# Two-layer diffusion step on one core: the second layer's feed-forward up product in seven block products instead of eight, and slabs of one size

## The chip, the cores and the metric

One core of a Trainium2 chip runs the whole program. The metric is the device time of one execution in microseconds (us), median of several runs. Engines: PE is TensorE (PEld its weight loads), DVE VectorE, ACT ScalarE, POOL GpSimd, SP the queue that issues DMAs.

## The reference, cut to what matters

A backbone of two layers works on 128 context and 512 latent tokens, 640 in all, of 1024 features. Each layer has attention, a state-space scan (SSD) and, at its end, the feed-forward part that the change is about:

```python
D_MODEL = 1024; SEQ = 128; DEC_SEQ = 512; DEPTH = 2; D_FF = 2816; FFN_CONV = 3
...
    x = x + g1 * (merged @ p['w_out'])
    h = modulate(x, sh2, sc2)
    u = dw_conv(h @ p['w_up'], p['ffn_conv_w'], p['ffn_conv_b'])
    u_val, u_gate = jnp.split(u, 2, axis=-1)
    x = x + g2 * ((jax.nn.silu(u_gate) * u_val) @ p['w_down'])
```

`w_up` is 1024 by 5632 (u_val and u_gate, 2816 each), and `dw_conv` is a convolution of width three over tokens, per feature. Inputs and outputs are float32.

## The kernel before, in words

All products run on PE in float32 split in two parts: `split` makes a rounded high part (a CAST on ACT) and the rest (a subtraction on DVE), and each product of two split operands takes three matmuls (high·high, high·low, low·high).

Nothing is issued where it is written. The functions record operations on tiles in a `Flow`, whose list scheduler then orders each engine's operations: an operation is taken when its dependences and buffers allow, among several by the rank of its class (`RANK`: "f" for the main stream, "d" for work done beside it, "m" for the modulation), and at equal rank as recorded. Each engine then runs its rows in that fixed order. So all instructions of the trace carry one line, L178 (L182 after), and a row is known by its tiles: `pf`, `p`, `pp` are PSUM banks, `wr`/`wh`/`wl` a raw weight tile and its high and low part, `slab` the large buffers for tokens, `tmp` smaller ones, `fw` the convolution's weights and biases.

Feature-major products (`feat_half`) hold a weight tile of 128 x 128 in PE and stream tokens: 640 tokens lie in 642 padded columns, in halves of 386 and 256. Token-major ones (`tok_major`) hold tokens and stream 512 columns of weights.

The feed-forward part has 22 feature tiles for u_val and 22 for u_gate. `up_item(p, jl)` is one **unit**: two tiles (a = 0, 1) of each matrix (s = 0 for u_val, 1 for u_gate), two halves: 8 groups of 24 matmuls. Behind a group `conv_in` takes it out of PSUM with two ACT rows; behind two, `conv_taps` adds the neighbours (two DVE rows of 642); for s = 1 `silu2` and a multiplication gate the pair, and a split writes the product into the g slabs. Units come in three stages, **up 0** (four units), **up 1** (four) and **up 2** (three), each followed by `down_item(p, 0)` and `(p, 1)`, together **down p**, which multiplies the gated features with `w_down` in 240 matmuls of 512 columns (180 in down 2). Weights of a unit are two tiles of 128 x 2048 (`w_feat`, 1 MB each), loaded and split by `wprep` two specs ahead, in rings of two `wr` and three each of `wh` and `wl`.

Ahead of up 0 stands `w_out_item`: per token tile it updates x, normalises it (`norm_tile`), transposes it on PE, and `norm_mod` scales, shifts and splits it into four slabs of two sizes that all units read. Slabs of a second kind (`slabd`, NSLABD = 5 of them) carry g, the scan's B and C, and other things.

Of the kernel before, what the change touches and what calls it, by code (L numbers as in the profile page):

```python
# [18 lines left out]
P = 128  # L19
# [9 lines left out]
NSLABD = 5  # L29
# [11 lines left out]
def _mask(dims, cache={}):  # L41
    """Bits of the free elements that an access pattern touches."""
# [299 lines left out]
def hybrid_step_kernel(  # L342
# [25 lines left out]
    def slab(h, shape, dt=F32):  # L368
        return flow.tile(slabs, shape, dt, f"slab{h}", nm("slab"), 2)
# [98 lines left out]
    def wprep(parts, wide=False):  # L468
        parts, scales = parts if isinstance(parts, tuple) else (parts, None)
# [32 lines left out]
    # token-major product: stationary tokens, moving weights of 512 columns  # L502
# [16 lines left out]
    # tokens in two parts: tiles 0 to 2 and tiles 3 and 4  # L519
    def part(i):  # L520
        return (0, col(i)) if i < 3 else (1, col(i) - HOFF[1])

    def tile_h(hT, i):
        h, o = part(i)
        return lambda a, kt: hT[a][h][:, kt, o:o + P]

    # tokens that wait in DRAM: two quads of feature tiles, in pieces of four, tile after tile
    def tok_load(src, q0):
# [3 lines left out]
        def load(n):  # L532
            for _ in range(n):
                i = len(tiles)
                while len(pieces) < 4 * i + 4:
                    h, k = (0, 6) if len(pieces) < 12 else (1, 4)
                    t = slab(h, [P, k, 4, P], F32R)
                    pieces.extend(t[:, j] for j in range(k))
# [33 lines left out]
    def norm_x(xh, xns, junk):  # L572
        """Both halves of a token tile over their root mean square."""
# [15 lines left out]
    def norm_mod(src, h, i, n, modT, hT, on_act):  # L589
# [8 lines left out]
        b, o = part(i)  # L598
        ks = slice(4 * n, 4 * n + 4)
        split(hT[0][b][:, ks, o:o + P], hT[1][b][:, ks, o:o + P], h)  # L600

    def norm_tile(x0, x1, t, i, modT, hT):
        """x0 and t are written over."""
        xns = [x0, t]
        norm_x([x0, x1], xns, t)
        for n in range(2):
            h = xns[n].rearrange("p (k t) -> p k t", k=4)
            norm_mod(norm_T(xns[n]), h, i, n, modT, hT, n == 0)

# [5 lines left out]
    def mw():  # L615
        """Of its own while attention holds the other buffers."""
# [35 lines left out]
    # the first shifts and scales, straight to features on partitions: columns of silu(cond) in two parts  # L652
    def mod_T_first(ws):
# [3 lines left out]
        for n in range(2):  # L657
            for m in range(2):
# [15 lines left out]
                # the two parts and the bias  # L674
# [36 lines left out]
    def conv_in(raw, cc, ps, h, w1, b):  # L711
        o = HOFF[h]
# [872 lines left out]
```

## Time and profile before

| what | value |
|---|---|
| median of 3 runs | 2858.98 us (2857.31 to 2859.09) |
| profiled execution, span | 2854.8 us |
| PE, PEld busy | 2816.5 us (99%), 2456.6 us (86%) |
| DVE busy | 2066.4 us (72%) |
| ACT busy | 1291.9 us (45%) |
| POOL busy | 90.5 us (3%) |
| chain of waits that ended last | PE 95%, DMA 3%, DVE 1%, ACT 1% |

The span runs from the first to the last instruction of the profiled execution; the time of a run holds a few microseconds around it. Busy time is an average over stages with different limits; a stage is read by windows of the trace, in which each engine's busy time, count of instructions and the clock granted to TensorE stand side by side (1.00 is 2.4 GHz, 0.50 is 1.2 GHz). A busy time of a row overlaps the start of the next one on its engine, so what a row costs its queue is read from start to start.

### The profile page before, as it was taken

The page shows a single profiled execution, that of the slowest core. Times are in us where ns is not written, and L with a number is a line of the kernel's source. Part 1 is how long each engine was busy: PE and PEld are TensorE (multiplying, and loading weights), DVE is VectorE, ACT ScalarE, POOL GpSimd, SP SyncE. Part 2 cuts the span into 40 slices and gives each one's busy share as a digit, 9 for nine tenths or more (in the row PEclk, how much of TensorE's full clock was granted, in tenths as well). Part 3 has the DMA queues.
Part 4 walks back from the last instruction along what each step waited for, and adds up shares of the span by engine and source line. Part 5 has one row for each costly group of instructions (what it writes and reads, how often), then busy time and mean ns, then how long its engine had stood idle before and what let it go on. Part 6 is the DMA issues. An engine that isn't in the chain of part 4 may idle for free.

```text
span 2854.8 us, 41191 instructions
## 1 busy us (share of the span) xinstructions
PE 2816.5 (99%) x15620; PEld 2456.6 (86%) x15620; DVE 2066.4 (72%) x2851; ACT 1291.9 (45%) x2255; POOL 90.5 (3%) x408
## 2 busy tenths in 40 slices
PE   6999999999999999999999999999999999999999
PEld 4898997877788898998979989887887888989898
DVE  7878775987799599997677666598779456545554
ACT  6454654445353453452444645544454325524342
POOL 1200000000000000000011000000000000000000
PEclk9999999999999999999999999999999999999999
DMA  7343444677868546455352223457667553252423
GB/s 262 100 125 126 126 151 143 225 247 245 275 219 275 180 136 215 167 175 180 98 168 85 94 95 100 155 199 251 220 235 258 203 175 132 86 166 65 155 84 111
DMA packets 309679, 478.45 MB, mean 168 GB/s; under 512 B 19808, under 2 KB 139792, under 8 KB 304360
## 3 DMA queue, kind: packets, MB, share of 16 engines
q1 hardware_dynamic: 309480, 475.81, 50.0%
q8 instruction: 123, 2.02, 0.3%
q14 instruction: 76, 0.62, 0.1%
HBM read 384.08 MB, written 91.65 MB: 167 GB/s over the span
## 4 chain that ended last, share of the span: by engine, by line
PE 95%; DMA 3%; DVE 1%; ACT 1%; issue 0%; SPq 0%; POOL 0%; DVEq 0%; ACTq 0%
PE pf L178 79%; PE p L178 10%; PE pp L178 4%; PE pq L178 1%; DMA tmp<-in_state_ssd_dram 1%; DMA slab<-in_w_mod_dram 0%; DVE tmp L178 0%; DMA ga<-tmp 0%; DVE wl L178 0%; DMA tmp<-in_x_prompt_dram 0%; ACT tmp L178 0%; SPq L178 0%; DMA slab<-in_q_norm_dram 0%; DVE slab L178 0%; ACT wh L178 0%
## 5 line engine op out<-in xcount | busy, mean ns | idle before, releaser
L178 PE MATMUL pf<-wh,slab 128*128 128x512 f32 x3920 | 1268.3, 400 | 5.9 <-ACT slab L178 2.5
L178 PE MATMUL pf<-slab,wh 128*128 128x256 f32 (+1 forms) x4416 | 980.2, 311 | 3.4 <-DVE slab L178 1.9
L178 PEld LDWEIGHTS pf<-wh,slab 128*128 128x128 f32 x3920 | 733.1, 189 | 174.4 <-issue 7.3
L178 PE MATMUL pf<-wl,slab 128*128 128x512 f32 x1960 | 780.7, 398 | 0.0
L178 PEld LDWEIGHTS pf<-slab,wh 128*128 128x128 f32 x4416 | 741.8, 189 | 12.0 <-issue 5.7
L178 PE MATMUL pf<-slab,wl 128*128 128x256 f32 (+1 forms) x2208 | 685.1, 310 | 0.0
L178 DVE TENSOR_TENSOR wl<-wr,wh 128x2048 fp32r<-128x2048 f32 (+1 forms) x156 | 350.7, 2248 | 145.3 <-ACT wh L178 144.5
L178 PEld LDWEIGHTS pf<-wl,slab 128*128 128x128 f32 x1960 | 369.5, 189 | 86.6 <-issue 6.0
L178 ACT CAST wh<-wr 128x2048 fp32r<-128x2048 f32 (+1 forms) x156 | 293.0, 1879 | 320.7 <-PE pf L178 302.4
L178 PEld LDWEIGHTS pf<-slab,wl 128*128 128x128 f32 x2208 | 415.9, 188 | 3.0 <-issue 0.2
L178 DVE SCALAR_TENSOR_TENSOR tmp<-tmp,fw,tmp 128x642 f32<-128x642 f32 x176 | 155.5, 885 | 80.5 <-ACT tmp L178 66.3
L178 PE MATMUL p<-tmp,slab 128*128 128x64 f32 (+1 forms) x976 | 209.8, 336 | 0.3 <-DVE tmp L178 0.3
L178 ACT ACTIVATE tmp<-tmp 128x642 f32<-128x642 f32 (+2 forms) x176 | 120.9, 687 | 179.1 <-DVE tmp L178 145.5
L178 ACT ACTIVATE tmp<-pf,fw 128x386 f32<-128x386 f32 (+1 forms) x176 | 109.0, 620 | 175.4 <-PE pf L178 172.2
L178 DVE TENSOR_TENSOR tmp<-pf,tmp 128x512 f32<-128x512 f32 x100 | 68.3, 688 | 132.1 <-PE pf L178 131.8
L178 PEld LDWEIGHTS p<-tmp,slab 128*128 128x128 f32 x976 | 136.0, 190 | 16.2 <-ACT tmp L178 4.6
L178 ACT COPY tmp<-pf 128x256 f32<-128x256 f32 (+3 forms) x296 | 127.5, 431 | 44.1 <-PE pf L178 43.7
L178 DVE TENSOR_TENSOR slab<-tmp,slab 128x512 fp32r<-128x512 f32 (+4 forms) x182 | 109.0, 634 | 42.9 <-ACT slab L178 42.7
L178 DVE SCALAR_TENSOR_TENSOR macc<-tmp,cT,macc 128x512 f32<-128x512 f32 x196 | 137.7, 743 | 1.2 <-DMA tmp<-in_w_mod_dram 1.2
L178 DVE TENSOR_TENSOR tmp<-tmp,tmp 128x512 f32<-128x512 f32 (+3 forms) x190 | 133.7, 705 | 3.0 <-DMA tmp<-sz 0.6
L178 PEld LDWEIGHTS p<-cst,tmp 128*128 128x128 f32 (+2 forms) x750 | 92.3, 141 | 40.6 <-issue 16.1
L178 PE MATMUL p<-cst,tmp 128*128 128x128 f32 (+2 forms) x750 | 121.0, 276 | 5.1 <-DMA tmp<-in_state_ssd_dram 4.4
(131 smaller groups left out, 2564.3 us busy)
## 6 DMA issues: line engine op xcount, KB each, us to landing
wr<-in_w_in_dram SPq DMA_DIRECT2D x60, 1024.0 KB
wr<-in_w_up_dram SPq DMA_DIRECT2D x44, 1024.0 KB
slab<-row SPq DMA_DIRECT2D x40, 1024.0 KB
tmp<-in_w_mod_dram SPq DMA_DIRECT2D x116, 256.0 KB
tmp<-xres SPq DMA_DIRECT2D x85, 256.0 KB
wr<-in_w_down_dram SPq DMA_DIRECT2D x20, 1024.0 KB
tmp<-xs SPq DMA_DIRECT2D x72, 256.0 KB
xres<-tmp SPq DMA_DIRECT2D x70, 256.0 KB
```

The source lines that it names most:

```text
L178: self.ops.append((lane, lambda: call(*args, **kw), self._cost(lane, fn, outs, ins, kw), deps, touched, self.cls))
```

## The change

In layer 1 (`WIN = (1,)`) every unit but the first forms its product in blocks: tokens in two parts of TH = 322 and TR = 320 columns, input features in two halves of 512, output features in the two tiles a = 0, 1. Two-by-two block products that take eight block multiplications are made with seven (`win_unit`, the Winograd form of Strassen's scheme): for each of the two matrices seven products of 12 matmuls of 322 columns. Before, a unit is 96 matmuls of 386 columns and 96 of 256; after, 168 of 322.

`Blocks` replaces the split tokens: it holds h raw, and splits four blocks (11, 12, 21, 22) and four sums (t1 to t4), in slabs of both kinds. `Sums` replaces a weight tile's split: of its four blocks a11, a12, a21, a22 it makes s1 to s4 by four DVE rows of 512, and splits seven blocks into two `wh`/`wl` pairs, the first with a11, a12, s1, s2, the second with s4, s3, a22. A unit therefore takes four of these pairs, from the same rings of three.

In `win_unit` bank a first gets a11·X11, which ACT copies out (p1c), then s2·t2 is added (copied as u2), then s3·t3 (u3); bank c gets s1·t1 (p5c), then s4·X22; a third bank gets a12·X21. DVE adds these into the two convolution inputs. The last product, a22·t4, is put off (`behind`, `catch_up`) into the next matrix's `win_unit`, behind its s1 product. ACT and DVE rows that free a bank are of a new class "u", ranked ahead of all others.

All slabs of the first kind have one size now (4 buffers), the second kind has 7 buffers for 5, with `dt_item`'s five arrays in one of them instead of in space of their own.

```diff
-NSLABD = 5
+NSLABD = 7
+WIN = (1,)
+TH = 322
+TR = COLS - TH
...
-        "pe": {"m": 0, "d": 1, "f": 2}, "act": {"f": 0, "d": 1, "m": 2}, "dve": {"f": 0, "d": 1, "m": 2},
+        "pe": {"m": 0, "d": 1, "f": 2}, "act": {"u": -1, "f": 0, "d": 1, "m": 2},
+        "dve": {"u": -1, "f": 0, "d": 1, "m": 2},
...
-    def slab(h, shape, dt=F32):
-        return flow.tile(slabs, shape, dt, f"slab{h}", nm("slab"), 2)
+    def slab(shape, dt=F32):
+        return flow.tile(slabs, shape, dt, "slab", nm("slab"), 4)
...
+    class Blocks:
+        def __init__(self):
+            self.R = [slabd([P, 4, PADW]) for _ in range(2)]
...
+            self.X = {k: slab([P, 2, 4, TH], F32R) for k in ("11", "21", "22")}
+            self.X["12"] = slabd([P, 2, 4, TH], F32R)
...
+        def sums(self):
+            tr = slabd([P, 2, 4, TH])
+            for k in ("t1", "t2", "t3"):
+                self.X[k] = slabd([P, 2, 4, TH], F32R)
+            self.X["t4"] = slab([P, 2, 4, TH], F32R)
+            dve.tensor_sub(tr[:, 0], self.raw("11"), self.raw("12"))
+            self.part("t1", tr[:, 0])
+            dve.scalar_tensor_tensor(tr[:, 1], tr[:, 0], -1.0, self.raw("22"), ALU.mult, ALU.subtract)
+            self.part("t2", tr[:, 1])
+            t3, t4 = self.raw("12"), self.raw("21")
+            dve.tensor_sub(t3, self.raw("22"), t3)
+            self.part("t3", t3)
+            dve.scalar_tensor_tensor(t4, tr[:, 1], -1.0, t4, ALU.mult, ALU.subtract)
+            self.part("t4", t4)
...
+            a11, a12, a21, a22 = v[:, 0, :, 0], v[:, 1, :, 0], v[:, 0, :, 1], v[:, 1, :, 1]
+            put(0, 0, 2, v[:, :, :, 0])
+            dve.tensor_add(s3, a11, a21)
+            dve.tensor_add(a21, a21, a22)
+            put(0, 2, 1, a21)
+            dve.tensor_add(s2, s3, a22)
+            put(0, 3, 1, s2)
+            dve.tensor_add(s4, s2, a12)
+            put(1, 0, 1, s4)
+            put(1, 1, 1, s3)
+            put(1, 2, 1, a22)
...
+    def product(ps, w, x, start):
+        wh, wl = w
+        for k in range(4):
+            for j, (w, b) in enumerate(((wh, 0), (wh, 1), (wl, 0))):
+                pe.matmul(
+                    ps, lhsT=w[:, k, :], rhs=x[:, b, k, :], start=start and k + j == 0, stop=k + j == 5,
+                    skip_group_check=not start,
+                )
...
+        product(a, W["a11"], X["11"], True)
+        now(act.copy, p1c, a)
+        product(c, W["s1"], X["t1"], True)
+        now(act.copy, p5c, c)
+        catch_up()
+        product(a, W["s2"], X["t2"], False)
+        now(act.copy, u2, a)
+        product(b, W["a12"], X["21"], True)
+        r0, c0 = bufs(0)
+        now(dve.tensor_add, r0[:, 1:1 + TH], p1c, b)
+        product(c, W["s4"], X["22"], False)
+        now(dve.tensor_add, r0[:, 1 + TH:1 + COLS], u2[:, 0:TR], c[:, 0:TR])
+        product(a, W["s3"], X["t3"], False)
+        now(act.copy, u3, a)
+        conv(0, r0, c0)
+
+        def rest():
+            product(a, W["a22"], X["t4"], False)
+            r1, c1 = bufs(1)
+            dve.scalar_tensor_tensor(r1[:, 1 + TH:1 + COLS], u3[:, 0:TR], -1.0, p5c[:, 0:TR], ALU.mult, ALU.subtract)
+            now(act.mul, r1[:, 1:1 + TH], a, -1.0)
+            conv(1, r1, c1)
+
+        behind.append(rest)
...
+            kar = slabd([P, 5, NT, 64])
...
         def w_out_item(n):
...
+                        if l in WIN and i == 2:
+                            S["h2"].part("11")
+                            S["h2"].part("21")
+                if l in WIN and n == 1:
+                    S["h2"].part("12")
+                    S["h2"].part("22")
+                    S["h2"].sums()
...
                 j = 8 * p + jl
-                add([w_feat(w_up, l, P * j, 256), w_feat(w_up, l, P * (NFF + j), 256)], up_item(p, jl))
+                us = [w_feat(w_up, l, P * j, 256), w_feat(w_up, l, P * (NFF + j), 256)]
+                if l in WIN and p + jl > 0:
+                    us = [lambda u=u: Sums(u) for u in us]
+                add(us, up_item(p, jl))
```

How the rows stand. In the rows a name's last number tells buffers apart. DVE before, one unit late in layer 1: two weight subtractions, then the rows of 642 for two feature pairs.

```order
L178 TENSOR_TENSOR wl_3897_4001<-wr_3895_3999,wh_3896_4000 128x2048
L178 SCALAR_TENSOR_TENSOR tmp_3888_3992<-tmp_3887_3991,fw_2148_2252,tmp_3888_3992 128x642 x2
L178 TENSOR_TENSOR wl_3900_4004<-wr_3898_4002,wh_3899_4003 128x2048
L178 SCALAR_TENSOR_TENSOR tmp_3892_3996<-tmp_3891_3995,fw_2148_2252,tmp_3892_3996 128x642 x2
L178 SCALAR_TENSOR_TENSOR tmp_3892_3996<-tmp_3891_3995,tmp_3892_3996 128x642
L178 SCALAR_TENSOR_TENSOR tmp_3902_4006<-tmp_3901_4005,fw_2148_2252,tmp_3902_4006 128x642
L178 TENSOR_TENSOR tmp_3892_3996<-tmp_3892_3996,tmp_3888_3992 128x642
L178 SCALAR_TENSOR_TENSOR tmp_3902_4006<-tmp_3901_4005,fw_2148_2252,tmp_3902_4006 128x642
L178 TENSOR_TENSOR slab_3877_3981<-tmp_3892_3996,slab_3875_3979 128x642
L178 SCALAR_TENSOR_TENSOR tmp_3906_4010<-tmp_3905_4009,fw_2148_2252,tmp_3906_4010 128x642 x2
L178 SCALAR_TENSOR_TENSOR tmp_3906_4010<-tmp_3905_4009,tmp_3906_4010 128x642
L178 TENSOR_TENSOR tmp_3906_4010<-tmp_3906_4010,tmp_3902_4006 128x642
```

In its place DVE now has some forty rows a unit. This is the end of the stretch between a unit's first weight subtraction (1024 columns) and the multiplication that gates the unit before, in up 1: `wr_3815_3919` is the raw weight tile two specs ahead, whose sums stand here.

```order
L182 TENSOR_TENSOR tmp_3821_3925<-wr_3815_3919 128x512
L182 SCALAR_TENSOR_TENSOR tmp_3829_3933<-tmp_3828_3932,fw_2144_2248,tmp_3829_3933 128x642
L182 TENSOR_TENSOR wr_3815_3919<-wr_3815_3919 128x4x128
L182 TENSOR_TENSOR tmp_3820_3924<-tmp_3821_3925,wr_3815_3919 128x512
L182 SCALAR_TENSOR_TENSOR tmp_3829_3933<-tmp_3828_3932,tmp_3829_3933 128x642
L182 TENSOR_TENSOR tmp_3822_3926<-tmp_3820_3924,wr_3815_3919 128x512
L182 TENSOR_TENSOR tmp_3830_3934<-tmp_3825_3929,p1_3827_3931 128x322
L182 TENSOR_TENSOR tmp_3829_3933<-tmp_3829_3933,tmp_3804_3908 128x642
L182 TENSOR_TENSOR slab_3789_3893<-tmp_3829_3933,slab_3787_3891 128x642
L182 TENSOR_TENSOR wl_3811_3915<-tmp_3814_3918,wh_3810_3914 128x512
```

Ahead of the gating row (`tmp_3829_3933<-tmp_3829_3933,tmp_3804_3908`) now stand four weight sums and the first sum out of a bank; before, the gating followed the convolution rows directly.

ACT in up 1, from the cast of that gated product to the next 1024-column weight cast; `pf_3823_3927` is bank a of the unit that PE is in, `wh_3816_3920` the first weight tile of the unit after it.

```order
L182 CAST slab_3787_3891<-tmp_3829_3933 128x642
L182 CAST wh_3810_3914<-tmp_3814_3918 128x512
L182 COPY tmp_3826_3930<-pf_3823_3927 128x322
L182 CAST wh_3810_3914<-tmp_3813_3917 128x512
L182 CAST wh_3810_3914<-wr_3807_3911 128x512
L182 COPY tmp_3834_3938<-pf_3832_3936 128x322
L182 ACTIVATE tmp_3831_3935<-tmp_3830_3934,fw_2144_2248 128x642
L182 COPY tmp_3826_3930<-pf_3823_3927 128x322
L182 COPY tmp_3834_3938<-pf_3833_3937 128x322
L182 CAST wh_3816_3920<-wr_3815_3919 128x1024
```

Behind the cast of the gated product stand a weight cast and the copy of u2 (`tmp_3826_3930<-pf_3823_3927`); before, the cast of the gated product stood between copies of whole groups, and no copy was followed by another product into the same bank.

## Rows read from the trace of the kernel before

**Rows 1.** The page: span, busy time of each engine, chain of waits by engine.
```profile
span 2854.8 us, 41191 instructions
...
PE 2816.5 (99%) x15620; PEld 2456.6 (86%) x15620; DVE 2066.4 (72%) x2851; ACT 1291.9 (45%) x2255; POOL 90.5 (3%) x408
...
PE 95%; DMA 3%; DVE 1%; ACT 1%; issue 0%; SPq 0%; POOL 0%; DVEq 0%; ACTq 0%
```

**Rows 2.** Windows, layer 1: up 0 without its first unit, down 0, up 1, up 2, one unit.
```profile
core 0: us, PE busy (x) PEld busy (x) DVE busy (x) ACT busy (x) POOL busy (x), PEclk, DMA share, GB/s
2416.60:2501.10 84.50, 84.50 (x584) 84.50 (x583) 54.64 (x54) 43.83 (x70) 1.53 (x24) 1.00 0.28 88
2501.10:2556.80 55.70, 55.70 (x243) 45.10 (x242) 23.84 (x27) 9.90 (x9) 0.38 (x6) 1.00 0.50 165
2556.80:2668.60 111.80, 111.80 (x770) 111.80 (x769) 63.68 (x62) 53.89 (x84) 1.66 (x26) 1.00 0.27 89
...
2724.40:2808.20 83.80, 83.80 (x577) 83.80 (x576) 46.36 (x46) 39.09 (x62) 1.22 (x18) 1.00 0.26 84
...
2584.71:2612.66 27.95, 27.95 (x195) 27.95 (x194) 16.30 (x16) 14.06 (x22) 0.51 (x8) 1.00 0.24 77
```

**Rows 3.** DVE's weight rows in that one unit: count, busy, mean ns, idle ahead.
```profile
L178 DVE TENSOR_TENSOR wl<-wr,wh 128x2048 fp32r<-128x2048 f32 x2 | 4.6, 2294 | 4.7 <-ACT wh L178 4.7
```

**Rows 4.** Instruction groups of ACT in that one unit.
```profile
L178 ACT CAST wh<-wr 128x2048 fp32r<-128x2048 f32 x2 | 3.8, 1911 | 2.3 <-PE pf L178 2.3
...
L178 ACT COPY tmp<-pf 128x386 f32<-128x386 f32 x4 | 1.9, 474 | 0.0
...
L178 ACT CAST slab<-tmp 128x642 fp32r<-128x642 f32 x2 | 1.5, 730 | 1.9 <-DVE tmp L178 1.8
```

**Rows 5.** Timeline of PE: first matmuls of one 386-, one 256-, one more 386-column half.
```profile
2584.71 0.52 PE L178 MATMUL pf<-slab,wh 128*128 128x386 f32 x2
...
2588.97 0.40 PE L178 MATMUL pf<-slab,wh 128*128 128x256 f32 x2
...
2591.70 0.52 PE L178 MATMUL pf<-slab,wh 128*128 128x386 f32 x2
```

**Rows 6.** Timeline of DVE, two stretches without idle time (start, busy, what).
```profile
2374.49 0.68 DVE L178 TENSOR_TENSOR tmp<-pf,tmp 128x512 f32<-128x512 f32 x1
2375.09 1.28 DVE L178 TENSOR_TENSOR slab<-tmp,slab 128x512 fp32r<-128x512 f32 x2
...
2416.61 2.29 DVE L178 TENSOR_TENSOR wl<-wr,wh 128x2048 fp32r<-128x2048 f32 x1 [1.31 <-ACT wh L178]
2418.82 0.82 DVE L178 SCALAR_TENSOR_TENSOR tmp<-tmp,tmp 128x642 f32<-128x642 f32 x1
2419.55 0.88 DVE L178 SCALAR_TENSOR_TENSOR tmp<-tmp,fw,tmp 128x642 f32<-128x642 f32 x1
2420.35 0.82 DVE L178 TENSOR_TENSOR tmp<-tmp,tmp 128x642 f32<-128x642 f32 x1
```

**Rows 7.** Timeline of ACT: released by the matmuls that end at 2588.97.
```profile
2589.17 0.68 ACT L178 ACTIVATE tmp<-pf,fw 128x386 f32<-128x386 f32 x1 [1.74 <-PE pf L178]
```

**Rows 8.** Chain of waits, end of w_out, layer 1: a hand-over, and the last transposes.
```profile
2386.04 0.14 issue
...
2397.55 1.06 PE p L178 x8
```

**Rows 9.** Windows: a stretch with PE idle, the next one, and another with idle time.
```profile
2383.20:2386.60 3.40, 1.72 (x8) 0.98 (x7) 3.40 (x5) 3.40 (x8) 0.88 (x1) 1.00 0.01 1
2386.60:2390.00 3.40, 3.40 (x13) 3.30 (x13) 3.00 (x6) 0.83 (x1) 0.90 (x5) 0.50 0.95 333
1438.50:1442.50 4.00, 1.56 (x8) 0.98 (x7) 2.56 (x3) 0.19 (x1) 0.00 (x0) 1.00 0.76 256
```

**Rows 10.** Windows: the scan phases of layer 0 and layer 1.
```profile
460.00:925.00 465.00, 461.86 (x2241) 372.48 (x2240) 385.30 (x511) 210.03 (x374) 1.59 (x4) 1.00 0.70 241
1820.00:2330.00 510.00, 507.81 (x2442) 409.77 (x2441) 376.88 (x485) 221.96 (x385) 1.60 (x4) 1.00 0.64 222
```

More of the change, by code (lines that the diff above doesn't have):

```diff
@@ L535, in load @@
                 while len(pieces) < 4 * i + 4:
-                    h, k = (0, 6) if len(pieces) < 12 else (1, 4)
-                    t = slab(h, [P, k, 4, P], F32R)
-                    pieces.extend(t[:, j] for j in range(k))
+                    t = slab([P, 5, 4, P], F32R)
+                    pieces.extend(t[:, j] for j in range(5))
                 for r in range(2):
@@ new lines, in hybrid_step_kernel, with __init__, put @@
+    class Sums:
+        def __init__(self, parts):
+            r, _ = wraw(parts, False)
+            v = r.rearrange("p (j k i c) -> p j k i c", j=2, k=4, i=2)
+            hl = [[flow.tile(wp, [P, 4, 4, P], F32R, n, nm(n), 3) for n in ("wh", "wl")] for _ in range(2)]
+            def put(t, o, n, src):
+                h, l = hl[t][0][:, o:o + n], hl[t][1][:, o:o + n]
+                src = src if n > 1 else src.unsqueeze(1)
+                split(h, l, src)
+            keepc = flow.cls
+            flow.cls = "d"
+            s2, s3, s4 = (t2((P, 4, P)) for _ in range(3))
+            flow.cls = keepc
+            a11, a12, a21, a22 = v[:, 0, :, 0], v[:, 1, :, 0], v[:, 0, :, 1], v[:, 1, :, 1]
[9 more added lines that the diff above has]
+            put(1, 2, 1, a22)
+            self.w = {n: (hl[t][0][:, o], hl[t][1][:, o]) for n, t, o in (
+                ("a11", 0, 0), ("a12", 0, 1), ("s1", 0, 2), ("s2", 0, 3), ("s4", 1, 0), ("s3", 1, 1), ("a22", 1, 2))}
@@ new lines, in product, with catch_up, win_unit, now @@
+    def product(ps, w, x, start):
[6 more added lines that the diff above has]
+                )
+    behind = []
+    def catch_up():
+        while behind:
+            behind.pop(0)()
+    def win_unit(W, X, bufs, taps, done):
+        W, X = W.w, X.X
+        a, c = psf()[:, 0:TH], psf()[:, 0:TH]
+        flow.cls = "d"
+        ta, tb = cv((P, 2, TH)), cv((P, 2, TH))
+        b = flow.tile(p1, [P, 512], F32, "p1", nm("p1"), 2)[:, 0:TH]
+        flow.cls = "f"
+        p1c, p5c, u2, u3 = ta[:, 0, 0:TH], ta[:, 1, 0:TH], tb[:, 0, 0:TH], tb[:, 1, 0:TH]
+        def now(fn, *args, **kw):
+            flow.cls = "u"
+            fn(*args, **kw)
+            flow.cls = "f"
+        def conv(k, raw, cc):
+            w0, w1, w2, bias = taps(k)
+            act.activation(cc, raw[:, 1:COLS + 1], AF.Identity, scale=w1, bias=bias)
+            conv_taps(raw, cc, w0, w2)
+            done(k)
+        product(a, W["a11"], X["11"], True)
[20 more added lines that the diff above has]
+        behind.append(rest)
@@ L597, in norm_mod @@
                 dve.tensor_scalar(h[:, k, :], src[:, k, :], sc, sh, ALU.mult, ALU.add)
-        b, o = part(i)
-        ks = slice(4 * n, 4 * n + 4)
-        split(hT[0][b][:, ks, o:o + P], hT[1][b][:, ks, o:o + P], h)
+        if not isinstance(hT, Blocks):
+            o = slice(col(i), col(i) + P)
+            split(hT[0][n][:, :, o], hT[1][n][:, :, o], h)
     def norm_tile(x0, x1, t, i, modT, hT):
@@ L972, in arr @@
                 return t2()[:, 0:n]
+            kar = slabd([P, 5, NT, 64])
+            kn = iter(range(5))
             def karr(tag):
-                return keep([P, NT, 64], F32, tag)
+                return kar[:, next(kn)]
             def fl(t):
@@ L1335, in fn @@
                     nq = 2 if 8 * p + 4 < NFF else 1
-                    S["g", p] = [[slabd([P, 4, PADW], F32R) for _ in range(nq)] for _ in range(2)]
+                    S["g", p] = [[slabd([P, 4, COLS], F32R) for _ in range(nq)] for _ in range(2)]
                 gs = S["g", p]
@@ L1369, in fn @@
             def fn(ws):
+                catch_up()
                 g = gate_bc(l, 1, n)
```

85 lines of the change are left out of this document (60 added, 25 removed).

## The prediction, made before the changed kernel was run

> **What bounds the kernel now.** I read the page first [rows 1]: TensorE (PE) is busy 99% of the 2854.8 us and the chain of waits is 95% PE, so most of the time is matmuls. The sum is made against that profiled execution; the median of the runs, 2858.98 us, lies 4.2 us above its span, and I add that back at the end. A change of 0.2%, 5.7 us, is about what a measurement of this kernel can tell from none.
>
> Then the windows by stage [rows 2]. In layer 1's up stages PE has no idle time at all; one unit of two feature pairs takes 27.95 us. DVE is busy 16.30 us of it and ACT 14.06, and the DVE's long weight rows wait 4.7 us per unit for a cast that itself waits for PE [rows 3, 4]. So before the change PE sets the pace and both other engines have slack. The stages are 84.50 us (up 0 without its first unit), 111.80 (up 1) and 83.80 (up 2).
>
> **What leaves PE.** A half of 24 matmuls of 386 columns takes 2588.97 − 2584.71 = 4.26 us, 177.5 ns each; 24 of 256 columns 2591.70 − 2588.97 = 2.73, 113.7 ns each [rows 5]. On the line between the two, 322 columns take 146 ns; I take 147 (bounds 143 and 149, for the shorter 320 and a cost per matmul that I can't see). Before, a unit is four times 6.99 = 27.96 us. After, it is 14 products of 12 matmuls: a product is 1.76 us and a unit 24.7. If PE stayed the bound, ten units would give back 10 × 3.26 = 33 us.
>
> **What DVE gets.** From two DVE stretches without idle time I take start-to-start times, which are what a queue that never waits needs [rows 6]: 2048 columns 2.21, 642 columns 0.73, 642 with per-partition scalars 0.80, 512 columns 0.60; so about 1.04 ns a column over a fixed part, which gives 1024 columns 1.14 and 322 or 320 columns 0.40. A unit's DVE rows become 8 sums and 10 subtractions of 512, 2 of 1024, 6 of 322/320, and the same 14 rows of 642 as before: 18 × 0.60 + 2 × 1.14 + 6 × 0.40 + 8 × 0.80 + 6 × 0.73 = 26.3 us. By the same times a unit of before is 2 × 2.21 + 8 × 0.80 + 6 × 0.73 = 15.2. So DVE, at 26.3, now passes PE at 24.7. Were that all, the gain would be (27.95 − 26.3) × 10 = 16.5 us and not 33.
>
> **What the order makes of it.** The engines take their rows in order, and the rows of a unit form a ring that closes once per unit. I followed it in the order of the changed program (the three places shown ahead):
> 1. DVE, from the 1024-column subtraction of a unit's first weight tile to just before the multiplication that gates the unit before: 2 × 1.14 + 15 × 0.60 + 4 × 0.40 + 6 × 0.80 + 4 × 0.73 = 20.6 us, and about 0.1 of waits.
> 2. That multiplication, 0.82, and 0.05 to hand over.
> 3. ACT: the cast of its result, and behind it, in the same queue, a 512-column cast and the copy of the partial sum u2 out of PSUM. A 642 cast is busy 730 ns, a 2048 one 1911 [rows 4], so 0.84 ns a column; less the tenth by which busy time overlaps the next row, 0.63 and 0.52; the copy of 386 columns is busy 474 ns, one of 322 some 420. Together 1.6.
> 4. PE, 0.14 later [rows 8], as DVE to PE cost before: s3 cannot add to the bank until u2 is copied. Then s3, the second matrix's s1, and the a22 product that was put off: 3 × 1.76 = 5.3.
> 5. The a22 product is the last to read a weight tile of a ring of three. ACT starts about 0.2 after PE ends [rows 7], but the last reader of that high part is one matmul before the end, so 0.05; the 1024 cast is 1.05 (by the same line); then DVE, 0.03, at step 1 again.
> The ring is 20.7 + 0.87 + 1.6 + 0.14 + 5.3 + 1.13 = 29.8 us: longer than 27.95 before, and longer than either engine's own work. In up 2 the 512 cast stands behind the copy, 29.3.
>
> PE then idles some 5 us per unit: one hole of about 4.3 us after s4, waiting for u2, and shorter ones.
>
> **The clock.** In the trace one stretch of 3.40 us at the end of w_out had PE busy 1.72, and in the next 3.40 us the granted clock was 0.50, the lower of its two levels (1.2 against 2.4 GHz), with 13 matmuls in it; a stretch of 4.00 us with 1.56 busy kept 1.00 [rows 9]. So a hole this size has cost the clock once and spared it once; mine is the larger (4.3 against 1.7 and 2.4 us idle), so I take the loss. Half speed for 3.40 us is 1.7 us of work, and it falls on s3, s1 and a22, which are steps of the ring: 1.65 us per turn, as some of it may lie after them.
>
> The Trainium skill, "TensorE: Matmul & The Clock Gate", section "HAM oscillation — how this bites in real kernels", speaks against the change in the same way: a loop whose matmuls pause between bursts starts each burst at the low clock, and pays that in every iteration. By that rule all turns lose it, by the row that kept 1.00 none does; the forecast stands on the row that lost it, without the rule.
>
> **The sum by stage.**
> - Up 1: nine products and 0.9 of waits up to the first a22, 16.8; three turns, 89.4; four products behind, 7.1: 113.3 against 111.8, **+1.5**.
> - Up 2: 16.8 + 2 × 29.3 + 7.1 = 82.5 against 83.8, **−1.3**.
> - Up 0: w_out's end gains, since the token splits of the last tile go away (PE waited there, and the clock fell [rows 9]: about 1.7 + 1.7 us). But DVE must make the eight token blocks: ten rows of 1288 columns, 14.1 us, after the last tile. That tile's transposes end at 2398.6 before [rows 8], 3.4 earlier now, and its eight copies and the rows about them take DVE to about 2397.2. Then come the ten rows, then 18.6 us of weight parts and convolutions and 0.8 of sums before the first Strassen unit's second half can start, with 1 us of waits 2431.7. Two products, 0.2: the first a22 ends at 2435.5. Two turns and 7.1: 2502.2 against 2501.1, **+1.1**.
> - Down 0, 1 and 2 start while the last gated slab is still on its way: two convolutions, the gate and a split, about 7 us behind PE with DVE behind too. 54 matmuls of 512 columns (0.232 each, from 55.70 over 240 [rows 2]) cover 12.5 us in the first two, 36 cover 8.4 in the last. I take 1.1 us each, **+3.3**, between 0 and 2.5 each.
> - The clock: 7 turns × 1.65 = **+11.6**.
> - The slabs of one size (seven of the second kind for five, four of the first) move rows only in the scan phases, where PE idles 3.1 and 2.2 us of 465 and 510 [rows 10]: 0, between −3 and +3. POOL's eight memsets a unit stay as they are, 0.51 us beside everything; the attention phases' order is the same.
> - The weights' DMAs are as many and as large; in a unit the queues are 0.24 busy [rows 2], and a longer unit lowers that: 0.
> Sum 1.5 − 1.3 + 1.1 + 3.3 + 11.6 = +16.2 us: 2854.8 + 16.2 + 4.2 = 2875 us.
>
> **Rivals.**
> - *The ring without the clock.* The holes leave the clock at 1.00, as the third of [rows 9] did. Then +4.6: 2864 us.
> - *Faster: the ring does not bind.* It decides at 27.95: below that a turn gains. It would take 1.9 us less on the ring, say if ACT's cast and copy came earlier, or DVE's 15 rows of 512 took 0.50 and not 0.60. With DVE the bound at 26.3: 2859.0 − 16.5 + 3 = 2845; with PE, 2859 − 33 + 1 = 2827. For it: DVE and PE both have less than 27.95 of own work. Against: every DVE time comes from stretches without idle time, and the row that each engine waits for is fixed by the order.
> - *Two low stretches per turn*, or one for the short holes as well: another 11.6 us, 2887 us.
> - *It doesn't do what it says*: the order shows 14 products of 12 matmuls of 322 in ten units, so I give this nothing.
>
> **How the numbers follow.** Forecast with the clock loss 0.52 (2868 to 2882 by its bounds: downs ±3.5, scans ±3, turn ±0.4 us each); ring alone 0.23; faster 0.13; two stretches 0.12. The time is that of the likeliest, 2875. The range leaves out the faster case, 0.13, and the far end of the two stretches, 0.05: 2856 to 2889. Slower by over 0.2% (above 2864.7): the forecast, the two stretches and nearly half of the ring alone, 0.74. Within 0.2%: the rest of that, and 0.01 of the faster case, 0.14. Faster: 0.12.
>
> **What would show it.** In the changed kernel's windows: up 1 at 119 us or so (113 without the clock loss, under 108 if I am wrong), PE busy under 24.9 per unit plus what the low clock adds, DVE some 27 to 28 busy of about 31; a low granted clock right behind each hole; in DVE's groups the 512 rows at 0.68 busy; in the waits, s3 released by ACT's copy, and the 1024 cast released by PE's `pf`. If the 1024 subtraction never waits, step 5 is wrong; if PE's holes are under 2 us, step 3 or 4 is.

## The result, and the profile after

The changed kernel takes 2889.39 us (median of 4 runs, 2885.59 to 2890.1) beside 2859.03 us for the kernel before on the same chip: 30 us more, a ratio of 1.0105 with a 95% interval of 1.0091 to 1.0119. The forecast was 2875 us and its range ended at 2889. The sign was right, and the time lies 0.4 us beyond the range's end; but the sum that led there was wrong in two terms, one far too small and one too large, which in part hid each other.

The page after has the same lines as [rows 1]: span, busy time, chain of waits.

```profile
span 2887.0 us, 41029 instructions
...
PE 2814.7 (97%) x15380; PEld 2445.4 (85%) x15380; DVE 2183.2 (76%) x3093; ACT 1329.7 (46%) x2333; POOL 92.2 (3%) x416
...
PE 88%; DMA 4%; DVE 4%; ACT 2%; issue 1%; SPq 1%; POOL 0%; DVEq 0%; ACTq 0%; POOLq 0%
```

PE's busy time has hardly fallen, though each unit in blocks has fewer columns, and the span is 32 us longer, so PE idles more: its part of the chain goes from 95% to 88%. Windows by stage, with the columns of [rows 2]: layer 0's scan phase, up 0 (here with its first unit), down 0, up 1, up 2, and one stretch within up 1 from a unit's first weight subtraction to the next unit's, called a **turn** below.

```profile
460.00:925.00 465.00, 450.08 (x2163) 360.31 (x2162) 370.39 (x494) 205.83 (x368) 1.58 (x4) 0.99 0.68 235
2411.30:2532.30 121.00, 112.59 (x721) 110.51 (x720) 107.66 (x147) 73.90 (x125) 4.90 (x38) 0.96 0.22 72
2532.30:2586.50 54.20, 54.20 (x235) 43.72 (x235) 34.30 (x46) 11.66 (x15) 0.51 (x8) 1.00 0.54 170
2586.50:2702.70 116.20, 107.06 (x681) 105.28 (x680) 96.06 (x139) 65.02 (x110) 1.52 (x24) 0.96 0.26 84
2756.80:2840.40 83.60, 78.90 (x512) 77.63 (x511) 69.16 (x101) 46.92 (x80) 1.02 (x16) 0.98 0.26 86
2636.10:2668.70 32.60, 28.15 (x170) 27.61 (x169) 26.86 (x40) 17.29 (x31) 0.51 (x8) 0.90 0.20 65
```

The first line stands against [rows 10]: in the same stretch of 465 us PE was busy 461.86 before and now 450.08. That is layer 0, where nothing is in blocks. The others stand against [rows 2]: in up 1 PE idles 9 us at a mean clock of 0.96, where before it idled none at 1.00.

Cut at the first matmul of each stage, the two traces (and all later ones) divide into six parts, in us:

| run | layer 0 to the scan | layer 0 scan | layer 0 up, down | layer 1 to the scan | layer 1 scan | layer 1 up, down, end |
|---|---|---|---|---|---|---|
| before | 393.8 | 577.1 | 549.3 | 291.2 | 564.3 | 470.1 |
| the change | 396.4 | 593.7 | 555.8 | 292.5 | 564.0 | 475.7 |
| no blocks, 7 slabs | 394.0 | 591.9 | 554.3 | 291.9 | 565.0 | 472.9 |
| no blocks, 6 slabs | 393.3 | 581.0 | 552.9 | 292.7 | 567.0 | 472.6 |
| rows at 64 bytes | 393.9 | 603.6 | 556.1 | 292.1 | 560.4 | 475.9 |
| no weight sums | 393.3 | 592.5 | 554.2 | 292.4 | 565.1 | 440.1 |
| useless matmuls | 396.8 | 593.4 | 556.2 | 292.4 | 563.8 | 471.1 |
| sums on POOL | 394.0 | 595.2 | 553.5 | 292.4 | 565.3 | 488.3 |
| blocks, 6 slabs | 394.4 | 577.2 | 554.5 | 292.7 | 566.8 | 476.0 |
| 6 slabs, sums on POOL | 393.9 | 578.4 | 553.5 | 292.8 | 569.9 | 483.2 |
| 6 slabs, a22 not put off | 396.1 | 578.7 | 553.1 | 292.8 | 566.4 | 460.6 |

(The first part starts 9 us into the span.) Of the 32 us between the spans only 5.6 arise in the part that has the blocks. The other 26.7 lie ahead of it, 16.6 of them in layer 0's scan phase and 6.5 in layer 0's up and down stages.

**Layer 0's scan phase.** PE's waits in 460 to 925 us have one large line (total, times, longest):

```profile
PE pf L182 <- DVE tmp L182: 8.5, 1, 8.5
```

The rows around it (start, us, what):

```profile
878.78 0.60 PE L182 MATMUL p<-cst,tmp 128*128 128x128 f32 x4
...
882.79 0.44 SPq L182 DMA_DIRECT2D y<-tmp  x1
...
888.73 0.33 SPq L182 DMA_DIRECT2D tmp<-y  x1
...
892.08 0.62 ACT L182 CAST slab<-tmp 128x512 fp32r<-128x512 f32 x1 [7.90 <-DMA tmp<-y]
892.90 0.68 DVE L182 TENSOR_TENSOR slab<-tmp,slab 128x512 fp32r<-128x512 f32 x1
893.50 0.68 DVE L182 TENSOR_TENSOR tmp<-pf,tmp 128x512 f32<-128x512 f32 x1
...
894.24 1.22 PE L182 MATMUL pf<-wh,slab 128*128 128x512 f32 x2 [8.45 <-DVE tmp L182]
```

PE transposes the scan's last result at 878.78. That result goes through DRAM: it is written (issued at 882.79, 5.92 us by the chain of waits) and read back (issued at 888.73) as tokens of the next product. ACT's cast of it waits 7.90 us for this, DVE's split stands behind the cast, and behind that in DVE's queue the row that empties a PSUM bank. PE has no matmul left at 885.8 and goes on at 894.24. The same place in the kernel before:

```profile
855.33 0.44 PE p L178 x4
855.77 20.20 PE pf L178 x87
875.97 0.44 PE pq L178 x4
876.40 3.71 PE pf L178 x16
```

There the scan's last matmuls (`p`, the same transposes) end at 855.8, and 20 us of other products follow, which cover the same round trip. In the changed order the transposes stand 21 us later in the phase, and from their end at 879.1 only 6.7 us of other products are left. The granted clock is 0.50 for 6.8 us from 890.4; PE works in 3.0 of them, about 1.5 us more.

**A turn of the ring.** DVE in up 1, from one unit's 1024-column subtraction to the next one's (start, us, what, idle before):

```profile
2636.09 1.83 DVE L182 TENSOR_TENSOR wl<-wr,wh 128x1024 fp32r<-128x1024 f32 x2 [2.50 <-ACT wh L182]
...
2652.57 0.69 DVE L182 TENSOR_TENSOR tmp<-tmp,wr 128x512 f32<-128x512 f32 x1
2653.17 0.69 DVE L182 TENSOR_TENSOR tmp<-wr 128x512 f32<-128x512 f32 x1
2653.77 0.88 DVE L182 SCALAR_TENSOR_TENSOR tmp<-tmp,fw,tmp 128x642 f32<-128x642 f32 x1
...
2657.51 0.83 DVE L182 TENSOR_TENSOR tmp<-tmp,tmp 128x642 f32<-128x642 f32 x1
...
2668.71 1.83 DVE L182 TENSOR_TENSOR wl<-wr,wh 128x1024 fp32r<-128x1024 f32 x2 [2.58 <-ACT wh L182]
```

32.62 us from 2636.09 to 2668.71, and the row waits 2.5 us each time for ACT's cast. The multiplication starts 21.4 after the first, where the prediction had 20.7. The chain within that turn:

```profile
2652.57 2.10 DVE tmp L182 x3
...
2654.75 1.07 ACT tmp L182 x2
2655.82 0.04 issue
2655.86 16.18 PE pf L182 x89
```

The first matmul behind the hole, on PE's timeline:

```profile
2655.86 0.90 PE L182 MATMUL pf<-slab,wh 128*128 128x322 f32 x2 [4.01 <-ACT tmp L182]
```

The hole on PE, 4.01 us, is there, but two products earlier than forecast: s2 waits for the copy p1c, which stands on ACT behind the `ACTIVATE` of the gate (both in the row at 2654.75), and that waits for DVE's convolution row. From 2655.1 the clock is at 0.50 for 6.8 us. DVE's rows are not quite the longest way there: at 2649.22 one of them waits 0.67 us for ACT, which the a22 product that ends at 2645.8 had held up.

### The profile page after: what moved, and what is told of

It reads as the page before. It is cut to its first block, busy times and chain, and to the rows that moved or that the text cites. A ratio compares the mean times of both kernels' runs of the same rounds, so it can differ in the third digit from the quotient of the medians.

```text
span 2887.0 us, 41029 instructions
## 1 busy us (share of the span) xinstructions
PE 2814.7 (97%) x15380; PEld 2445.4 (85%) x15380; DVE 2183.2 (76%) x3093; ACT 1329.7 (46%) x2333; POOL 92.2 (3%) x416
## 4 chain that ended last, share of the span: by engine, by line
PE 88%; DMA 4%; DVE 4%; ACT 2%; issue 1%; SPq 1%; POOL 0%; DVEq 0%; ACTq 0%; POOLq 0%
PE pf L182 73%; PE p L182 10%; PE pp L182 3%; DVE tmp L182 2%; PE pq L182 1%; DVE slab L182 1%; ACT tmp L182 1%; DMA slab<-row 1%; DVE wl L182 1%; DMA mw<-in_w_mod_dram 1%; ACT wh L182 1%; DMA tmp<-xs 1%; SPq L182 1%; DMA slab<-in_w_mod_dram 0%; DMA tmp<-in_state_ssd_dram 0%
## 5 line engine op out<-in xcount | busy, mean ns | idle before, releaser
L182 PE MATMUL pf<-slab,wh 128*128 128x386 f32 (+3 forms) x4096 | 934.9, 315 | 18.6 <-ACT tmp L182 17.0
L182 PEld LDWEIGHTS pf<-slab,wh 128*128 128x128 f32 x4096 | 699.3, 191 | 28.8 <-ACT tmp L182 18.8
L182 PE MATMUL pf<-slab,wl 128*128 128x386 f32 (+3 forms) x2048 | 644.6, 315 | 4.9 <-DVE wl L182 4.9
L182 DVE TENSOR_TENSOR wl<-wr,wh 128x2048 fp32r<-128x2048 f32 (+2 forms) x196 | 355.8, 1821 | 108.2 <-ACT wh L182 107.8
L182 ACT CAST wh<-wr 128x2048 fp32r<-128x2048 f32 (+2 forms) x196 | 300.5, 1537 | 266.2 <-PE pf L182 249.0
L182 PEld LDWEIGHTS pf<-slab,wl 128*128 128x128 f32 x2048 | 389.8, 190 | 9.9 <-DVE wl L182 6.9
L182 ACT COPY tmp<-pf 128x256 f32<-128x256 f32 (+5 forms) x296 | 126.9, 434 | 65.8 <-PE pf L182 65.6
L182 DVE TENSOR_TENSOR slab<-slab,slab 128x512 f32<-128x512 f32 (+2 forms) x137 | 120.3, 901 | 46.3 <-ACT slab L182 34.7
L182 ACT ACTIVATE tmp<-pf 128x512 f32<-128x512 f32 (+2 forms) x130 | 72.3, 556 | 147.4 <-PE pf L182 139.9
L182 DVE TENSOR_TENSOR tmp<-tmp,slab 128x512 f32<-128x512 f32 (+3 forms) x254 | 123.1, 518 | 9.7 <-DMA tmp<-xs 8.0
```

Of the source, the lines that this page charges most:

```text
L182: self.ops.append((lane, lambda: call(*args, **kw), self._cost(lane, fn, outs, ins, kw), deps, touched, self.cls))
```

## The experiments

First the question whether the loss comes from the slabs or the blocks.

**No blocks, seven slabs** (`WIN = (1,)` becomes `WIN = ()`).

> The change with its slabs, but no unit in blocks (no layer in WIN). Theory A (the slabs cost the time: the order of layer 0's scan phase and the halves that now lie in a tile of 642 columns): the scan phase of layer 0 stays at 593 us (577 before), each up stage of both layers keeps 256-column matmuls at 119 ns (114 before), 11 units x 96 x 5.7 ns = 6 us more in layer 1: about 2859 + 27 + 6 = 2892 us, slower than the change itself. Theory B (the blocks cost it, the stages ahead of them only by chance or by contention from work of layer 1): 2859 to 2865 us.

Measured 2882.0 us, ratio 1.0087 (1.0071 to 1.0102). Theory A holds in kind: 22 of the 30 us are there without any block. It is 10 us less than A gave: the last part lost 2.8 us and not 6, the parts ahead of it 21.3 and not 27. The median of the change is 7 us above this run's; in the traces the part that has the blocks differs by 2.8.

**No blocks, six slabs** (also `NSLABD = 6`).

> As the run with no unit in blocks, but with six slabs of the second kind and not seven: with the one that now holds the decay arrays, that is five for everything else, as before the change. A1 (the number of slabs decides the scan phase, by the order that the scheduler then makes): the 8.45 us wait of PE at 886 us is gone and layer 0's scan phase is back at 577 to 579 us, so 14 to 16 us faster than with seven, about 2876 us; the halves of 256 columns stay at 119 ns. A2 (the place of the arrays or the layout does it): the scan phase stays at 593 us, the time within 3 us of the run with seven.

Measured 2871.5 us, ratio 1.0054 (1.0036 to 1.0072); the scan phase 581.0 us without the long wait. A1 holds, with 4 us of the phase left.

**Rows at 64 bytes.**

```diff
-HALF = (386, 256)
-HOFF = (0, 386)
+HALF = (384, 258)
+HOFF = (0, 384)
...
-            pair = [slab([P, 4, COLS], F32R) for _ in range(2)]
+            pair = [slab([P, 4, 656], F32R) for _ in range(2)]
```

> The change, with the token tile's rows 656 columns apart and not 642, and halves of 384 and 258, so that every row and half starts at a multiple of 16 columns (64 bytes). A (where a half starts in its tile sets the rate): a 258-column matmul of layer 0's up stages takes 114 to 115 ns, 384 columns 170 to 177, and the three up stages of layer 0 fall by 5 us or more; in all 2882 us or less, if the new order of the attention phases costs nothing. Rival (the number of tiles, or the tile's size, sets it): 258 columns at 119 to 121 ns, the time within 3 us of the change's 2889.

Measured 2894.2 us, ratio 1.0127 (1.0112 to 1.0142). 258 columns took 119.8 ns: a start at 64 bytes does not restore the rate. The order changed with the halves, and the scan phase grew to 603.6 us.

**No weight sums** (plain blocks stand in their place, so this run doesn't compute the reference's products; subtractions, casts and matmuls are as many).

```diff
-            s2, s3, s4 = (t2((P, 4, P)) for _ in range(3))
...
-            dve.tensor_add(s3, a11, a21)
-            dve.tensor_add(a21, a21, a22)
             put(0, 2, 1, a21)
-            dve.tensor_add(s2, s3, a22)
-            put(0, 3, 1, s2)
-            dve.tensor_add(s4, s2, a12)
-            put(1, 0, 1, s4)
-            put(1, 1, 1, s3)
+            put(0, 3, 1, a22)
+            put(1, 0, 1, a12)
+            put(1, 1, 1, a11)
```

> The change without the four weight sums of a matrix (8 DVE rows of 512 columns a unit, 4.8 us); plain blocks stand in their place, so the products are not those of the reference; subtractions, casts and matmuls are as many. Ring theory (a turn of 32.6 us goes through DVE's rows, ACT's casts and copies and five PE products, and the low clock lies on it): a turn falls by 4.8 us and by the low clock (1.7 us) where the hole of 4 us closes, to 26 to 28 us; five turns give 20 to 30 us, so 2860 to 2869 us, and no low clock in the up stages of layer 1. Rival (PE's own order and the copies out of PSUM set the holes, DVE is only late beside them): the holes stay, under 8 us gained, 2881 us or more.

Measured 2850.6 us, ratio 0.9972 (0.9961 to 0.9983): 38.8 us less than the change, 35.6 of it in the last part. Up 1 in windows:

```profile
2567.80:2668.40 100.60, 100.60 (x677) 100.39 (x676) 81.68 (x116) 65.67 (x110) 1.52 (x24) 1.00 0.29 98
```

PE is busy throughout, at full clock: 25.15 us a unit, which is the 14 products of 12 at 149.7 ns. So 4.8 us of DVE a unit hold back all that the blocks save on PE. The ring theory holds; the gain went past its figure, since a turn fell not to 26 to 28 us but to PE's own 25. The scheduler orders the rows anew in such a run, so their order may have a part in it.

Next, what the low clock costs, and whether the sums can go elsewhere.

**Useless matmuls ahead of the hole** (in `win_unit`, for the first matrix of the five units that have a hole of 2.7 to 4.0 us).

```diff
         catch_up()
+        if first:
+            product(ps1()[:, 0:TH], W["a11"], X["11"], True)
         product(a, W["s2"], X["t2"], False)
```

> The change with 12 useless matmuls of 322 columns, into a bank of their own, in each of the five turns that have a hole of about 4 us on PE (two in up 0, two in up 1, one in up 2); DVE's and ACT's rows stand exactly as in the change. They stand ahead of the hole and take 1.8 us of it. Clock theory (the low clock behind a hole lies on the ring): if the clock then stays at 1.00, the 23.8 us at half speed in layer 1's up stages go, which is 11.9 us of work; 8 to 12 us faster than the change, 2877 to 2881 us. If the clock falls as before: 2889, within 2 us. Rival (PE's time counts as such, the ring has no slack for it): 5 x 1.8 us slower, about 2898 us.

Measured 2884.8 us, ratio 1.0095 (1.008 to 1.011): 4.6 us less than the change, though the two ratios' intervals overlap. In the traces, one execution of each, PE's busy time at half clock in layer 1's up stages fell from 22.4 to 6.4 us, that is 8 us of work, and the last part by 4.6 us. The turn:

```profile
2634.13 1.83 DVE L182 TENSOR_TENSOR wl<-wr,wh 128x1024 fp32r<-128x1024 f32 x2 [1.80 <-ACT wh L182]
...
2665.40 1.82 DVE L182 TENSOR_TENSOR wl<-wr,wh 128x1024 fp32r<-128x1024 f32 x2 [2.13 <-ACT wh L182]
```

31.27 us for 32.62. So the low clock lies on the ring, but about half of it is absorbed by the rest of the ring; sixty matmuls that compute nothing made the part that has them no longer, but 4.6 us shorter. The holes that were left at 2.15 us kept the clock, those of 2.9 lost it; but a hole's size alone doesn't tell, for in the run with a22 not put off (below) one of 2.58 us kept it and one of 1.85 lost it. The Trainium skill ("TensorE: Matmul & The Clock Gate", section "HAM oscillation — how this bites in real kernels") says that such a loop pays in each iteration; the trace of the change agrees (a low stretch behind each of the five holes, 3.4 or 6.8 us), and this run shows that what it pays is less than the work lost.

**Sums on POOL** (the four `dve.tensor_add` of `Sums` become `pool.tensor_tensor`, with 1200 ns in the scheduler's cost).

> The change with the four weight sums of a matrix on POOL and not on DVE (rows of 512 columns, eight a unit), nothing left out. Ring theory: as in the run without these sums, if a row of POOL takes under 2 us (eight a unit, 25 us) and does not slow DVE: layer 1 from the end of w_out falls by some 30 us, about 2852 to 2860 us. Rival (POOL is too slow, or slows DVE's rows while it works): sums late, PE waits for the second weight tile; anything from 2870 to over 2900 us.

Measured 2905.5 us, ratio 1.0162 (1.0147 to 1.0177): the rival. Groups of instructions of POOL (whole run), then of DVE in the same run and in the change, both in up 1 (busy, mean ns, idle before):

```profile
L182 POOL TENSOR_TENSOR tmp<-tmp,wr 128x512 f32<-128x512 f32 x40 | 64.1, 1602 | 2.3 <-DVE wl L182 1.3
```

```profile
L182 DVE TENSOR_TENSOR wl<-tmp,wh 128x512 fp32r<-128x512 f32 x18 | 23.9, 1355 | 5.5 <-ACT wh L182 5.5
...
L182 DVE TENSOR_TENSOR tmp<-tmp,p 128x322 f32<-128x322 f32 x6 | 2.9, 480 | 1.6 <-issue 1.6
```

```profile
L182 DVE TENSOR_TENSOR wl<-tmp,wh 128x512 fp32r<-128x512 f32 x21 | 13.8, 687 | 3.5 <-ACT wh L182 3.5
```

POOL's sum takes 1.6 us, and beside it DVE's subtractions with two operands in SBUF take 1355 ns on the mean for 687. The row with an operand in PSUM keeps its time (480, 484 in the change). This is the behaviour that the Trainium skill states ("SBUF — State Buffer", section "SBUF: two separate sides"): a POOL instruction and a DVE one with two SBUF inputs lock each other out of a shared port.

**Blocks, six slabs** (`NSLABD = 6`, five of the first kind, t3 moved to those; `tr` becomes `self.raw("11")`, written over in place).

> The change with six slabs of the second kind and five of the first, the sums of token blocks formed in place. Slab theory (the number of second-kind slabs sets the order of layer 0's scan phase, and with it the wait of 8.5 us at its end): as with six and no blocks, the scan phase at 577 to 583 us and not 593; the up stages of layer 1 as in the change; 2876 to 2880 us. Rival: the order falls out otherwise with five of the first kind, another wait in the scan phase, 2885 us or more.

Measured 2871.7 us, ratio 1.0048 (1.0031 to 1.0065). The scan phase is at 577.2 us. PE's waits from 860 to 980 us:

```profile
PE pf L182 <- DVE tmp L182: 0.4, 1, 0.4
```

**Six slabs and sums on POOL.**

> Both of the last two: six slabs of the second kind, and the weight sums on POOL. If both theories hold the gains add up: 2889 - 10 - 30 to 35, some 2845 us, faster than before the change by 10 to 15 us. If POOL's rows are slow: 2865 to 2890 us.

Measured 2882.5 us, ratio 1.0082 (1.0067 to 1.0097). The slabs' gain adds; POOL's loss is there too, 10.8 us against the run with six slabs alone (16.1 with seven).

Then the ring itself was shortened.

**a22 not put off** (on top of six slabs).

```diff
+        e = ps2()[:, 0, 0:TH] if odd else ps1()[:, 0:TH]
         product(a, W["a11"], X["11"], True)
...
-        catch_up()
...
+        product(e, W["a22"], X["t4"], True)
         product(a, W["s3"], X["t3"], False)
-        now(act.copy, u3, a)
         conv(0, r0, c0)
-
-        def rest():
-            product(a, W["a22"], X["t4"], False)
-            r1, c1 = bufs(1)
-            dve.scalar_tensor_tensor(r1[:, 1 + TH:1 + COLS], u3[:, 0:TR], -1.0, p5c[:, 0:TR], ALU.mult, ALU.subtract)
-            now(act.mul, r1[:, 1:1 + TH], a, -1.0)
-            conv(1, r1, c1)
-
-        behind.append(rest)
+        r1, c1 = bufs(1)
+        now(act.copy, u3, a)
+        now(dve.scalar_tensor_tensor, r1[:, 1:1 + TH], u3, -1.0, e, ALU.mult, ALU.subtract)
+        dve.scalar_tensor_tensor(r1[:, 1 + TH:1 + COLS], u3[:, 0:TR], -1.0, p5c[:, 0:TR], ALU.mult, ALU.subtract)
+        conv(1, r1, c1)
```

> The run with six slabs and sums in place, in which also the a22 product isn't put off: it goes into a bank of its own (one of the attention's, idle here), and DVE subtracts it (one row of 322 more per matrix, two ACT rows fewer). Then the last reader of a unit's second weight tile is s3 and not a22 behind the next matrix's s1. Ring theory: a turn loses two PE products (3.6 us at full clock) of its 32.6, so 27.5 to 29 us, DVE's own rows being 27.1; holes under 2 us and no low clock; five turns give 18 to 25 us against the run with six slabs, 2847 to 2854 us. Rival (DVE's and ACT's order sets the turn, PE's products lie beside it): under 5 us gained, 2867 us or more.

Measured 2856.9 us, ratio 0.9997 (0.9987 to 1.0007): no different from before, 14.8 us less than with a22 put off. The 1024-column rows, then up 1 and the turn between these rows in windows:

```profile
2610.95 1.83 DVE L182 TENSOR_TENSOR wl<-wr,wh 128x1024 fp32r<-128x1024 f32 x2
...
2640.56 1.82 DVE L182 TENSOR_TENSOR wl<-wr,wh 128x1024 fp32r<-128x1024 f32 x2
```

```profile
2567.50:2675.10 107.60, 102.38 (x674) 101.35 (x673) 97.92 (x145) 62.46 (x102) 1.53 (x24) 0.98 0.28 90
...
2610.95:2640.56 29.61, 26.56 (x178) 26.04 (x177) 28.29 (x44) 17.44 (x31) 0.51 (x8) 1.00 0.29 96
```

The subtraction no longer waits (no bracket), so the ring is open at that place; the turn is 29.6 us, and DVE is busy 28.3 of it, PE 26.6. In such a turn DVE's rows are now the bound. The gain fell short of the figure, since I had DVE at 27.1 a unit and its remaining waits at nothing.

**Where a row of 256 columns lies.** Five runs with other places for the halves. First rows 768 columns apart, the half of 256 ahead, no blocks, six slabs:

> No unit in blocks, six slabs, the token tile's rows 768 columns apart, and halves of 256 (first) and 386, so that each 256-column row starts at a multiple of 1024 bytes, as before the change. If that start sets the rate, 256 columns take 114 ns in the up stages, 386 at 176 to 178: a unit at 27.95 us, the up stages of layer 0 back within 1 us of 120.0, 115.4 and 84.6, some 6 us less than the run with six slabs and no blocks (2871). If not, 119 ns, and the stages stay at 121, 117 and 86; then the tile that the half lies in, not its start, is what is left.

Measured 2873.0 us, ratio 1.0053 (1.0037 to 1.0069). Starts of 24 matmuls of 256 columns and of the half behind, in layer 0's up stages, in the change and in this run:

```profile
1205.02 0.40 PE L182 MATMUL pf<-slab,wh 128*128 128x256 f32 x2
...
1207.88 0.52 PE L182 MATMUL pf<-slab,wh 128*128 128x386 f32 x2
```

```profile
1204.94 0.39 PE L182 MATMUL pf<-slab,wh 128*128 128x256 f32 x2
...
1207.66 0.51 PE L182 MATMUL pf<-slab,wh 128*128 128x386 f32 x2
```

2.86 against 2.72 us, 119 against 113 ns: the place changes the rate. But the order of the halves gave layer 0's scan phase its long wait back (594.0 us, PE waits 10.7). Then the same half at rows 656 columns apart, with the blocks and without:

> The run with a22 not put off and six slabs, with halves of 256 (first) and 386 in token tiles whose rows lie 656 columns apart, so that each 256-column row starts at a multiple of 64 bytes and ends at one, and no farther. Lines theory (a matmul pays for the 64-byte lines that its row touches: 256 columns from such a start touch 16, from another 17; the 258 columns of the earlier run touched 17 from a good start): 256 columns at 113.5 to 114.5 ns in the up stages of layer 0, these 4 to 6 us shorter, the whole some 2851 us, faster than before the change by 0.2%. Rival (a start at some larger multiple is needed, as both fast layouts had): 119 ns, the whole at 2857 us. In either case the scan phases may differ by a few us, since the scheduler orders them anew.

> The same token tiles and halves with no unit in blocks and six slabs. Lines theory: up stages of both layers at before's times within 1 us (120, 115.4, 84.6 and 111.8, 83.8), so 5 to 7 us less than the 2871 us of the six-slab run without blocks, if the newly ordered scan phases cost the same; 2864 to 2866 us. Rival: 119 ns and 2871 us.

Measured 2870.9 us (1.0048, 1.0036 to 1.0061) and 2887.7 us (1.011, 1.0095 to 1.0126), 256 columns at 118 ns in both: the lines theory falls. The second of them differs from the run before in the rows' distance alone, 656 columns for 768. The scan phase is 595 us in both. Last, the halves packed one behind the other in a tile, every instruction in the order of the run with a22 not put off, then also with tiles that start alike:

> The run with a22 not put off, with the same order of every instruction; only the place of the token halves in their tiles differs: the four rows of 256 columns lie one behind the other (1024 bytes apart) at the tile's start, the four of 386 behind them. If rows at one and the same phase of a larger multiple are what the fast layouts had in common, 256 columns take 113 to 115 ns in the up stages of layer 0, its three stages fall from 121.6, 117.2 and 85.9 by 1.5 to 2 us each, the whole by some 5 us to 2851 to 2853 us, faster than before the change by 0.2%. If the rate goes with the base of each tile (they differ in steps of 64 bytes), some groups of 256 columns run at 113 and others at 119 ns, the whole 2 to 4 us less. Rival (the place isn't it): 119 ns, 2857 us.

> As the last run, the order of every instruction the same, with the token tiles 10496 bytes long and not 10304, so that all of them start at the same place within 256 bytes. In the last run the high and the low part of the tokens lay in tiles whose starts differ by 64 bytes or a multiple; in both fast layouts they stood alike. If that is it, 256 columns at 113 to 115 ns, the three up stages of layer 0 shorter by 1.5 to 2 us each, the whole at some 2851 us. If not, 118 ns as in the last run, 2856 us, and the cause stays open.

Measured 2856.1 us (0.9996, 0.9987 to 1.0005) and 2859.7 us (1.0002, 0.9993 to 1.0011), 256 columns at 118 and 119 ns. Neither start is it. What the two fast layouts share beyond this stays open, and the layout isn't all of it: in the kernel before, nine of the ten unbroken series of 20 to 24 such matmuls in layer 0's and layer 1's parts ahead of the scan took 117.6 to 117.7 ns, with tokens laid out as in the up stages. None of the versions that leave nothing out beats the kernel before.

## Why the prediction was right in sign and wrong in its sum

- **"The slabs of one size ... 0, between −3 and +3"** is the step that failed most. The parts ahead of layer 1's up stages measured +26.7, and +21.3 with no block in the program. I took PE's idle time in the scan phases, 3.1 and 2.2 us, as the bound; but that bounds what a new order can give, not what it can cost. The order there did change, and a round trip through DRAM lost its cover. The runs with six slabs (581.0 and 577.2 for 591.9 and 593.7) show the number of slabs to be its cause here. The runs with reversed halves show that another change of order opens the same hole with six (10.1 to 10.7 us), so it isn't the number as such.
- In the same step, 4 to 6 us in layer 0's up stages went unseen, since I costed the new place of the 256-column rows at nothing. Shown is that the place changes the rate; which property of it does is not.
- **"Seven turns"** was the other. A turn at the ring's length needs the sums of a unit that follows in the same stage, so the last one of each stage is none. From the a22 product of one unit's first matrix to the next unit's (ACT's row behind that product, `ACTIVATE tmp<-pf`) the trace has 31.5 and 27.2 us in up 0, 31.6, 32.6 and 27.2 in up 1, 31.6 and 27.2 in up 2: four turns, and three stretches of 27.2 with no hole over 0.5 us. Those three alone take 12 us off the part's sum of 16.2; measured 5.6.
- **Right:** the price of a product (149 ns for 147 a matmul), DVE's rows to the hundredth (0.60 and 0.80 from start to start), DVE above PE, and a ring that is longer than either and that closes through the weight tile that a22 frees. Taking out its DVE rows, or two of its products, shortened it. That a turn came to 32.6 for 31.45 is in part luck: PE goes on 19.8 us after the subtraction and not 23.3, since it waits for an earlier row of DVE; but from there to the cast five products and the low clock take 11.8 us and not 7.0.
- **Right in kind:** the hole of 4 us and the low clock behind it. Four holes of 3.8 to 4.0 us were at s2 (behind p1c), not s3 (behind u2); a fifth, of 2.7, at the start of up 0 waited for a part of a weight. The work lost at the low clock came near the forecast by luck, 11.2 us for 11.6: five low stretches, two of them of 6.8 us, for seven of 3.4. By the run with useless matmuls about half of what such a stretch takes is absorbed.
- **"Downs +3.3"** did not come: down 0 and 1 take 54.2 and 54.1 us for 55.7 and 55.8, as the first eight matmuls of each run among those of the last a22 product, in the up stage; nothing was late. With these 3.3 off as well the part's sum is some 0.7, and 5.6 were measured: the first a22 of up 0 ends some 3.5 us later than forecast (2465.7, less the 26.7 lost ahead, for 2435.5), and turns are up to 1.2 us longer.
- **The rival on the other side** (DVE the bound, 2845 us) named the way to gain, a shorter ring; the run that opened the ring took 3 us off a turn and 9.5 off the last part against before, and came to no difference, as 11.5 us of the slabs' costs ahead of it remained.

## What to carry to other kernels

A saving on the busiest engine must be paid for in rows on the next one, and when two in-order engines and a ring of buffers form a loop, the loop's length, and not either engine's sum, is the price: follow it row by row, and count how many times it really closes. A change of buffer counts under a list scheduler is a change of order everywhere: the idle time there now bounds what it may give, not what it may cost; look for the long round trips, and for the work that covers each of them now.

## What the runs showed of the hardware

- The place in SBUF of a matmul's moving rows changed its rate: in the up stages 256 columns took on the mean 113 to 114 ns in two layouts and 118 to 119 in all others that were tried, with 64-byte starts among the slow ones. The same layout also ran at 117.7 ns in other stages of the kernel before.
- Useless matmuls ahead of a hole of 4 us took PE's busy time at half clock from 22.4 to 6.4 us in layer 1's up stages, and the part that has them was 4.6 us shorter.
- A POOL sum of 512 columns, 1.6 us, doubled the time of DVE rows with two SBUF operands (687 to 1355 ns) and left those with one in PSUM as they were.
